# An even stream of ada rows, columns made in the middle of a block, scaled squares, and end products in two parts

## The chip, the cores and the metric

The kernel runs on one core of one Trainium2 chip. The metric is the time of one execution on the device, in microseconds. TensorE multiplies, VectorE and ScalarE work elementwise, GpSimd (POOL) does small operations and issues some DMAs, SyncE (SP) issues the others. Each engine takes its instructions in the order in which they were put into its queue and waits at an instruction until what it needs is there.

## The reference

One transformer layer on 256 tokens of width 2048, in float32. Nine vectors of 2048 (shift, scale and gate for three sublayers) come from `ada`. Each sublayer normalises its input, scales and shifts it, computes, and adds the result with a gate before a second normalisation.

```python
def _modulate(x, shift, scale):
    return _layernorm(x) * (1 + scale) + shift

def _swiglu(h, w_in, w_out):
    gate, up = jnp.split(h @ w_in, 2, axis=-1)
    return (jax.nn.silu(gate) * up) @ w_out

# in _layer
ada = (jax.nn.silu(c) @ w_ada + b_ada)[:, None, :]
sh1, sc1, g1, sh2, sc2, g2, sh3, sc3, g3 = jnp.split(ada, N_ADA, axis=-1)
h = _swiglu(_modulate(x, sh1, sc1), ffn1_w_in, ffn1_w_out)
x = _layernorm(ALPHA * x + 0.5 * (1 + g1) * h, ln1_g, ln1_b)
h = _token_mixer(_modulate(x, sh2, sc2), w_in, ...)
x = _layernorm(ALPHA * x + (1 + g2) * h, ln2_g, ln2_b)
h = _swiglu(_modulate(x, sh3, sc3), ffn2_w_in, ffn2_w_out)
x = _layernorm(ALPHA * x + 0.5 * (1 + g3) * h, ln3_g, ln3_b)
```

## The kernel before

Every matrix is split into a high part (`hi`, rounded to the fast matmul format) and the rest (`lo`). `split` makes them: ScalarE casts, VectorE subtracts (L145, L146). `mm3` then issues three products for one (L391 to L393). The 256 tokens are two row tiles of 128, a = 0 and 1. `res` holds the running x.

**The first stage** (the loop from L897) multiplies the modulated x with 24 column groups of `ffn1_w_in`, twelve of them in each of four phases j = 0 to 3. A phase uses the 512 input features 4j to 4j + 3 (in units of 128). A block n of a phase is one column group: 48 matmuls in two halves h = 0 and 1 (`first_in`, L809). Blocks other than the last add their result to `hT` on VectorE, or copy it there on ScalarE in the phase that is the first for them. The last block of a phase holds its sums in PSUM for the next phase.

The next phase needs the shift and scale of its 512 features. These are sums over 16 row blocks of `w_ada`, 512 KB each: POOL issues the load (`ar`, three buffers), VectorE multiplies by silu(c) and adds (L160; L158 for the first of them, which only multiplies). The sums lie in `acc` for j = 1 and 3 and in a part of `gate` for j = 0 and 2. `next_ada` does this in steps of two rows. At the end it transposes the sums on TensorE (L786), reduces them to columns on VectorE (L788) and adds the bias (L789). `modulate_both` (L307) normalises the 512 features on ScalarE, transposes them (L317), applies the columns on ScalarE (L322), and makes the parts `xhi` (ScalarE, L325) and `xlo` (VectorE, L327). A step of `next_ada` runs before block n for all n but 4 and 9; the one before block 11 makes the columns and finishes the modulation.

The order within an engine's queue isn't the order of the text alone. A planner issues, at each point of its own forecast, the instruction that stands first in the text among those that it takes to be ready. `tc.issue_after` puts an instruction behind a named one, and `manual_schedule` keeps VectorE in the order of the text.

**Between sublayers** (`boundary`, L572, used after the first and the second sublayer) the last output columns of both row tiles are multiplied (`last_products`), in two column halves of 256: `o` and `oh`. `add_up` adds them to x with the gate (L469 to L479, where L475 reads `oh`). Then `row_std`, `ln_affine` and `ln_stats` make the first normalisation and the mean and variance for the next one: `ln_affine` sums x in three pieces on VectorE (L541) and the squares of x minus the mean of the first piece on ScalarE (L545), with sums 7, 8 and 9. `ln_stats` puts mean and variance together on VectorE and takes the inverse root on POOL (`inv_root`, L271). POOL also multiplies it with minus the mean (L566). `modulate_tile` normalises (L339 on ScalarE; L337 on VectorE for the first tile alone), transposes (L343), applies the columns (L350, L353) and splits (L359, L360). The first products of the next sublayer (`mo` or `ge`, L664) begin with `xf` and unsplit weights.

Of the kernel before, what the change touches and what calls it, by code (L numbers as in the profile page):

```python
# [7 lines left out]
F32 = mybir.dt.float32  # L8
F32R = mybir.dt.float32r
AF = mybir.ActivationFunctionType  # L10
ALU = mybir.AluOpType
# [36 lines left out]
def layer_kernel(  # L48
# [282 lines left out]

    def modulate_tile(v, a, k0, nk, rs, xT, xs=None, on_v=False):
        ts_ = slice(a * P, (a + 1) * P)
        n = npool.tile([P, nk * P], F32, tag="n", bufs=2, name=f"n_{ntag()}")
        r = res[:, a, k0 * P:(k0 + nk) * P]
        if on_v:
            V.tensor_scalar(out=n, in0=r, scalar1=rs[:, 0:1], scalar2=rs[:, 1:2], op0=ALU.mult, op1=ALU.add)  # L337
        else:
            S.activation(n, r, AF.Identity, bias=rs[:, 1:2], scale=rs[:, 0:1])  # L339
# [82 lines left out]
    def out_proj(w, rows, nk, tag, npump, finish, before=None, turn=0, nheld=3, spare=None):  # L422
# [11 lines left out]
        for width in (1024, 512, 512):  # L434
# [16 lines left out]

            def last_products(a):
                half[a, 0] = mm_tile(f"oh_{tag}{a}")
                args = held[:-kn] + (kept if a else []) + held[-kn:]
                k0 = args[0][0] if a and kept and nu == nheld + 1 else None
                body, end = args[:-4], args[-4:]
                ends = end[0][0], end[-1][0]
                with tc.issue_after(last[0].ins) if a else nullcontext():
                    products(a, body, k0, None)
                    products(a, end, None, ends[1], w=256)  # L460
                    last.append(products(a, end, *ends, outs=half, c=256, w=256))

# [69 lines left out]
    def ln_affine(a, rs, mv, lgb, sums, sq):  # L532
# [6 lines left out]
        for i, (c0, c1) in enumerate(((0, 512), (512, 1280), (1280, 2048))):  # L539
# [3 lines left out]
            if i == 0:  # L543
                V.tensor_scalar_mul(sums[:, 4:5], sums[:, 0:1], -4.0 / D)
            S.activation(sq[:, :c1 - c0], r, AF.Square, bias=sums[:, 4:5], accum_out=sums[:, 7 + i:8 + i])  # L545
            yield


    def ln_stats(out_, sums, tag):
# [8 lines left out]
        yield  # L558
        V.tensor_scalar_add(s[2], s[2], EPS)
        yield 1  # L560
        V.tensor_scalar(out=s[6], in0=s[7], scalar1=s[8], scalar2=s[9], op0=ALU.add, op1=ALU.add)
        yield
        V.tensor_scalar(out=s[6], in0=s[6], scalar1=1.0 / D, scalar2=s[2], op0=ALU.mult, op1=ALU.add)
        yield
        inv_root(out_[:, 0:1], s[6])
# [6 lines left out]
    def boundary(products, add_up, st, lgb, v, tag, xT, entry, nk):  # L572
# [4 lines left out]
        with tc.manual_schedule(engines={mybir.EngineType.DVE}):  # L577
            products(0)
            products(1)
            for _ in add_up(0):  # L580
# [4 lines left out]
            for _ in aff[0]:  # L585
                pass
            together(lns[0])
            together(lns[0])
            m = [[modulate_tile(v, a, k, 2, mr[a], xT, xs if k < 6 else None, a + k == 0) for k in range(0, 8, 2)]
                 + [modulate_tile(v, a, k, 2, mr[a], xT) for k in range(8, nk, 2)] for a in range(2)]  # L590
            m0, m1 = m
            next(m0[0])
            next(m0[1])
            for _ in add_up(1):
# [166 lines left out]

    def next_ada(j):
        src = pair_cols(0, j)
        if j % 2:
            acc = ap.tile([P, 2, 512], F32, tag="acc", name=f"acc0_{j}")
        else:
            acc = gate[:, :1024].rearrange("p (v n) -> p v n", v=2)
        rows = []
        for k in range(0, KD + 2, 2):
            with behind(modulated[0]):  # L770
                for raw in rows:
                    ada_acc(acc, raw, k - 2 + rows.index(raw))
            rows = []
            for h in range(2 if k < KD else 0):
                raw = ap.tile([P, 2, 512], F32, tag="araw", bufs=3, name=f"ar0_{j}_{k + h}")
                G_.dma_start(raw, src[(k + h) * P:(k + h + 1) * P])
                rows.append(raw)
            if k == 10:
                mb = modulate_both(0, j, rs0, xT)
            if k in (10, 12):  # L780
                next(mb)
            yield
        js = slice(4 * j, 4 * j + 4)
        cps = aux_tile(f"cp{j}"), mm_tile(f"cq{j}")
# [4 lines left out]
        V.tensor_tensor(out=scsh[:, 0:2, js], in0=scsh[:, 0:2, js], in1=bcol[:, 0:2, js], op=ALU.add)  # L789
        for _ in mb:  # L790
            pass
        yield

# [14 lines left out]

    def first_in(j, n, i, ws):  # L809
        gu, q = i % 2, i // 2  # L810
# [5 lines left out]
        ws = list(ws)  # L816
        for h in range(2):
            for k, hi, lo in ws:
                for b, ps in enumerate(pss):
# [72 lines left out]
    with tc.manual_schedule(engines={mybir.EngineType.DVE, mybir.EngineType.Activation}):  # L892
        next(fa)
    ada["left"] = [ada_gate(2, 0, 0.5), ada_gate(2, 1, 0.5), *(ada_pair(3, j) for j in range(4)), ada_pair(6, 0),
                   ada_pair(6, 1), ada_gate(5, 0, 1.0), ada_gate(5, 1, 1.0), ada_pair(6, 2), ada_pair(6, 3),
                   ada_gate(8, 0, 0.5), ada_gate(8, 1, 0.5)]
    for j in range(4):  # L897
        fa = next_ada(j + 1) if j < 3 else load_mixer_smalls()
        for n, i in enumerate(order_of(j)):
            second = n == 1 and j == 0  # L900
            with behind(fence0[-1] if second else None), behind(high[0] if second else None):
                w = list(ws if n + j == 0 else first_w(j, i))
            for _ in range(n not in (4, 9)):
                next(fa, 0)
            with behind(fence0[-1] if second else None):
                fence0.append(first_in(j, n, i, w))
            if j == 3 and n > 2:
                pump(R_F)
# [597 lines left out]
```

## Time and profile before

| what | value |
|---|---|
| three runs | 1924.88, 1921.06, 1924.22 us; median 1924.22 |
| the profiled execution | 1923.22 us, its span 1921.5 us |
| TensorE, matmuls and weight loads | 1875.2 us and 1719.2 us busy |
| VectorE | 1463.2 us busy |
| ScalarE | 940.4 us busy |
| POOL | 56.8 us busy |
| granted TensorE clock | 0.998 |

The span runs from the first to the last instruction; the execution's own time is 1.7 us more. Matmuls overlap each other in the profile, so a wait of TensorE is best seen in the starts of the weight loads (PEld), one for each matmul. In rows of the timeline, the first column is the start, the second the duration in us, and brackets name the idle time before it and what ended it. In rows of the chain, the columns are start, duration, and what ran.

### The profile page before, as it was taken

What the parts mean: (1) busy time and instruction counts of PE and PEld (TensorE: products, weight loads), DVE (VectorE), ACT (ScalarE), POOL (GpSimd) and SP (SyncE); (2) the same over time, 40 slices, a digit from 0 to 9 for tenths busy, and PEclk for the clock granted to TensorE, in tenths of its full rate; (3) what the DMA queues carried; (4) which work ended last, traced back from release to release, by engine and by line L of the source; (5) the groups of instructions that cost most, each with busy time, mean ns of one, the idle gap of its engine ahead of it and who ended that gap; (6) DMA issues with size and microseconds to landing.
All of it is one profiled execution on the core that took longest, in us unless ns stands there. A gap on an engine that the chain in (4) does not pass through costs nothing.

```text
span 1921.5 us, 32164 instructions
## 1 busy us (share of the span) xinstructions
PE 1875.2 (98%) x13101; PEld 1719.2 (89%) x13101; DVE 1463.2 (76%) x1766; ACT 940.4 (49%) x1310; POOL 56.8 (3%) x89
## 2 busy tenths in 40 slices
PE   3999999999999999999999999999999999999997
PEld 3999999999988888698999886999999999988886
DVE  6789979777778899678787887777775654555776
ACT  5554354344354454745665544565444443544562
POOL 1211100000000000000000000000000000000000
PEclk9999999999999999999999999999999999999999
DMA  9988869999888787489878884997687656655552
GB/s 363 365 305 310 325 218 315 315 308 336 285 319 318 268 310 263 154 301 321 280 260 286 307 293 148 335 304 265 226 277 257 224 185 198 237 189 188 197 196 89
DMA packets 295867, 510.89 MB, mean 266 GB/s; under 512 B 10882, under 2 KB 159010, under 8 KB 294696
## 3 DMA queue, kind: packets, MB, share of 16 engines
q1 hardware_dynamic: 287944, 480.53, 73.4%
q0 software_dynamic: 7776, 28.32, 4.2%
q8 instruction: 102, 1.67, 0.4%
q14 instruction: 45, 0.37, 0.1%
HBM read 506.71 MB, written 2.10 MB: 265 GB/s over the span
## 4 chain that ended last, share of the span: by engine, by line
PE 89%; DVE 5%; DMA 3%; ACT 1%; issue 1%; SPq 0%; POOL 0%; DVEq 0%; ACTq 0%; POOLq 0%
PE gu_f L393 8%; PE gu_f L391 8%; PE gu_f L392 8%; PE o_f L391 8%; PE o_f L393 8%; PE o_f L392 8%; PE s L392 4%; PE s L393 4%; PE s L391 4%; DMA ar<-in_w_ada_dram 2%; PE fh L393 2%; PE fh L392 2%; PE fh L391 2%; PE fs L392 1%; PE fs L393 1%; PE fs L391 1%
## 5 line engine op out<-in xcount | busy, mean ns | idle before, releaser
L160 DVE SCALAR_TENSOR_TENSOR acc<-ar,csil,acc 128x1024 f32<-128x1024 f32 x240 | 307.5, 1281 | 33.0 <-DMA ar<-in_w_ada_dram 32.6
L392 PE MATMUL gu_f<-xlo_f,hi_f2i 128*128 128x256 f32 x768 | 212.1, 276 | 0.0
L393 PE MATMUL gu_f<-xhi_f,lo_f2i 128*128 128x256 f32 x768 | 212.1, 276 | 0.0
L391 PE MATMUL gu_f<-xhi_f,hi_f2i 128*128 128x256 f32 x768 | 212.1, 276 | 0.0
L391 PE MATMUL s<-xhi_f,hi_s 128*128 128x256 f32 x752 | 208.7, 278 | 0.7 <-ACT xhi_f L325 0.7
L392 PE MATMUL s<-xlo_f,hi_s 128*128 128x256 f32 x752 | 208.4, 277 | 0.2
L393 PE MATMUL s<-xhi_f,lo_s 128*128 128x256 f32 x752 | 207.8, 276 | 0.0
L146 DVE TENSOR_TENSOR lo_f2i<-raw_f2i,hi_f2i 128x1024 fp32r<-128x1024 f32 x96 | 117.6, 1225 | 99.8 <-ACT hi_f2i L145 99.8
L391 PE MATMUL gu_f<-xhi_f,hi_f1i 128*128 128x256 f32 x640 | 176.8, 276 | 0.0
L393 PE MATMUL gu_f<-xhi_f,lo_f1i 128*128 128x256 f32 x640 | 176.8, 276 | 0.0
L392 PE MATMUL gu_f<-xlo_f,hi_f1i 128*128 128x256 f32 x640 | 176.7, 276 | 0.0
L145 ACT CAST hi_f2i<-raw_f2i 128x1024 fp32r<-128x1024 f32 x96 | 100.8, 1050 | 137.4 <-PE gu_f L392 125.5
L145 ACT CAST hi_s<-raw_s 128x1024 fp32r<-128x1024 f32 x94 | 98.0, 1053 | 116.1 <-PE s L392 76.2
L392 PEld LDWEIGHTS gu_f<-xlo_f,hi_f2i 128*128 128x128 f32 x768 | 144.2, 188 | 0.1
L391 PEld LDWEIGHTS gu_f<-xhi_f,hi_f2i 128*128 128x128 f32 x768 | 144.2, 188 | 0.1
L393 PEld LDWEIGHTS gu_f<-xhi_f,lo_f2i 128*128 128x128 f32 x768 | 144.2, 188 | 0.0
L391 PEld LDWEIGHTS s<-xhi_f,hi_s 128*128 128x128 f32 x752 | 141.2, 188 | 1.3 <-ACT xhi_f L325 1.1
L392 PEld LDWEIGHTS s<-xlo_f,hi_s 128*128 128x128 f32 x752 | 141.3, 188 | 0.8 <-DVE xlo_f L327 0.5
L393 PEld LDWEIGHTS s<-xhi_f,lo_s 128*128 128x128 f32 x752 | 141.2, 188 | 0.0
L145 ACT CAST hi_f1i<-raw_f1i 128x1024 fp32r<-128x1024 f32 x80 | 83.4, 1050 | 116.6 <-PE gu_f L392 79.0
L145 ACT CAST hh<-hT 128x512 fp32r<-128x512 f32 x126 | 77.4, 621 | 124.6 <-PE o_f L392 124.4
L146 DVE TENSOR_TENSOR lo_f2o<-raw_f2o,hi_f2o 128x1024 fp32r<-128x1024 f32 x86 | 105.3, 1225 | 43.2 <-ACT hi_f2o L145 43.1
(503 smaller groups left out, 5433.5 us busy)
## 6 DMA issues: line engine op xcount, KB each, us to landing
ar<-in_w_ada_dram SPq DMA_DIRECT2D x240, 512.0 KB, 5.7
raw_f2i<-in_ffn_w_in_dram SPq DMA_DIRECT2D x48, 1024.0 KB, 5.1
raw_s<-in_ffn_w_in_dram SPq DMA_DIRECT2D x47, 1024.0 KB, 6.9
raw_f1o<-in_ffn_w_out_dram SPq DMA_DIRECT2D x44, 1024.0 KB, 7.5
raw_f2o<-in_ffn_w_out_dram SPq DMA_DIRECT2D x44, 1024.0 KB, 5.2
raw_f1i<-in_ffn_w_in_dram SPq DMA_DIRECT2D x40, 1024.0 KB, 7.5
ar<-in_w_ada_dram POOLq DMA_DIRECT2D x48, 512.0 KB, 6.7
raw_mxo<-in_w_out_dram SPq DMA_DIRECT2D x16, 1024.0 KB, 7.8
```

The source lines that it names most:

```text
L145: S.copy(hi, src)
L146: V.tensor_tensor(out=lo, in0=src, in1=hi.bitcast(F32), op=ALU.subtract)
L160: ins = V.scalar_tensor_tensor(out=acc, in0=raw, scalar=csil[:, k:k + 1], in1=acc, op0=ALU.mult, op1=ALU.add)
L391: PE.matmul(o, ah, bh, start=start, stop=False)
L392: PE.matmul(o, ah, bl, start=False, stop=False)
L393: return PE.matmul(o, al, bh, start=False, stop=stop)
```

## The change

Four things:

- The row loads and sums of phases 1 to 3 are one stream of 48 rows (`ada_stream`). A step issues the load of one row and the sum of the row two before it. Before a block one or two steps run: in phase 0 1, 1, 2, 2, 1, 2, 2, 1, 2, 2, 2, 1, and later two before every third block.
- The columns of the next phase are made between the two halves of block 10 (`middle`) and no longer before block 11. The normalisation and the transposes of its features stand before blocks 7 and 8 (they stood before 6 and 7), the rest of the modulation before block 11, as it did.
- The squares are scaled by 1/D within the activation. Their sums 7 and 8 are then put together with the variance's other terms on VectorE ahead of the wait, and POOL adds sum 9 just ahead of the root. The first normalised tile is (x + minus mean) times the root on VectorE, which does not use the product of L566.
- In `boundary` the end products of row tile 1 come in two parts: first all but the second column half, then, behind the normalisation and transposes of the first tile, the second half (`oh`).

```diff
-    def modulate_tile(v, a, k0, nk, rs, xT, xs=None, on_v=False):
+    def modulate_tile(v, a, k0, nk, rs, xT, xs=None, mean=None):
...
-        if on_v:
-            V.tensor_scalar(out=n, in0=r, scalar1=rs[:, 0:1], scalar2=rs[:, 1:2], op0=ALU.mult, op1=ALU.add)
+        if mean is not None:
+            V.tensor_scalar(out=n, in0=r, scalar1=mean, scalar2=rs[:, 0:1], op0=ALU.add, op1=ALU.mult)
...
-            def last_products(a):
-                half[a, 0] = mm_tile(f"oh_{tag}{a}")
+            def last_products(a, parts=(0, 1)):
+                if 0 in parts:
+                    half[a, 0] = mm_tile(f"oh_{tag}{a}")
...
-                    products(a, body, k0, None)
-                    products(a, end, None, ends[1], w=256)
-                    last.append(products(a, end, *ends, outs=half, c=256, w=256))
+                    if 0 in parts:
+                        products(a, body, k0, None)
+                        products(a, end, None, ends[1], w=256)
+                    if 1 in parts:
+                        last.append(products(a, end, *ends, outs=half, c=256, w=256))
...
-                V.tensor_scalar_mul(sums[:, 4:5], sums[:, 0:1], -4.0 / D)
-            S.activation(sq[:, :c1 - c0], r, AF.Square, bias=sums[:, 4:5], accum_out=sums[:, 7 + i:8 + i])
+                V.tensor_scalar_mul(sums[:, 4:5], sums[:, 0:1], -4.0 * D ** -1.5)
+            S.activation(sq[:, :c1 - c0], r, AF.Square, bias=sums[:, 4:5], scale=D ** -0.5, accum_out=sums[:, 7 + i:8 + i])
...
-        V.tensor_scalar_add(s[2], s[2], EPS)
+        V.tensor_scalar(out=s[6], in0=s[7], scalar1=s[2], scalar2=EPS, op0=ALU.add, op1=ALU.add)
+        yield
+        V.tensor_tensor(out=s[6], in0=s[6], in1=s[8], op=ALU.add)
         yield 1
-        V.tensor_scalar(out=s[6], in0=s[7], scalar1=s[8], scalar2=s[9], op0=ALU.add, op1=ALU.add)
-        yield
-        V.tensor_scalar(out=s[6], in0=s[6], scalar1=1.0 / D, scalar2=s[2], op0=ALU.mult, op1=ALU.add)
-        yield
+        G_.tensor_tensor(out=s[6], in0=s[6], in1=s[9], op=ALU.add)
         inv_root(out_[:, 0:1], s[6])
...
             products(0)
-            products(1)
+            products(1, (0,))
...
             next(m0[0])
+            products(1, (1,))
             next(m0[1])
...
-    def next_ada(j):
...
+    def ada_stream():
         rows = []
+        for r in range(3 * KD + 2):
+            if r >= 2:
+                with behind(modulated[0]):
+                    ada_acc(*rows.pop(0))
+            if r < 3 * KD:
+                j, k = 1 + r // KD, r % KD
+                if k == 0:
+                    sums0[j] = (ap.tile([P, 2, 512], F32, tag="acc", name=f"acc0_{j}") if j % 2 else
+                                gate[:, :1024].rearrange("p (v n) -> p v n", v=2))
+                raw = ap.tile([P, 2, 512], F32, tag="araw", bufs=3, name=f"ar0_{j}_{k}")
+                G_.dma_start(raw, pair_cols(0, j)[k * P:(k + 1) * P])
+                rows.append((sums0[j], raw, k))
             yield
...
+    def columns0(j):
+        acc, js = sums0[j], slice(4 * j, 4 * j + 4)
         cps = aux_tile(f"cp{j}"), mm_tile(f"cq{j}")
...
-    def first_in(j, n, i, ws):
+    def first_in(j, n, i, ws, middle=None):
...
         for h in range(2):
+            if h and middle:
+                middle()
...
+    rows0, smalls = ada_stream(), load_mixer_smalls()
     for j in range(4):
-        fa = next_ada(j + 1) if j < 3 else load_mixer_smalls()
...
-            for _ in range(n not in (4, 9)):
-                next(fa, 0)
+            for _ in range((1, 1, 2, 2, 1, 2, 2, 1, 2, 2, 2)[n] if j == 0 and n < 11 else 1 + ((n - 11) % 3 == 2)):
+                next(rows0, 0)
+            if j == 3:
+                next(smalls, 0)
+            elif n == 7:
+                mb = modulate_both(0, j + 1, rs0, xT)
+                next(mb)
+            elif n == 8:
+                next(mb)
+            elif n == 11:
+                for _ in mb:
+                    pass
...
-                fence0.append(first_in(j, n, i, w))
+                fence0.append(first_in(j, n, i, w, (lambda: columns0(j + 1)) if n == 10 and j < 3 else None))
```

More of the change, by code (lines that the diff above doesn't have):

```diff
@@ L588, in boundary @@
             together(lns[0])
-            m = [[modulate_tile(v, a, k, 2, mr[a], xT, xs if k < 6 else None, a + k == 0) for k in range(0, 8, 2)]
+            m = [[modulate_tile(v, a, k, 2, mr[a], xT, xs if k < 6 else None, None if a + k else sums[0][:, 5:6]) for k in range(0, 8, 2)]
                  + [modulate_tile(v, a, k, 2, mr[a], xT) for k in range(8, nk, 2)] for a in range(2)]
@@ L760, in first_ada @@
         yield
-    def next_ada(j):
[L763 to L767, printed above, removed]
-        rows = []
[L769 to L781, printed above, removed]
+    def ada_stream():
+        rows = []
+        for r in range(3 * KD + 2):
[10 more added lines that the diff above has]
+                rows.append((sums0[j], raw, k))
             yield
-        js = slice(4 * j, 4 * j + 4)
+    sums0 = {}
+    def columns0(j):
+        acc, js = sums0[j], slice(4 * j, 4 * j + 4)
         cps = aux_tile(f"cp{j}"), mm_tile(f"cq{j}")
@@ L789, in next_ada @@
         V.tensor_tensor(out=scsh[:, 0:2, js], in0=scsh[:, 0:2, js], in1=bcol[:, 0:2, js], op=ALU.add)
-        for _ in mb:
-            pass
-        yield
     NS = 12
```

## The prediction

> **What bounds the kernel now.** I read the page first (busy times, the chain that ended last), then the table of stretches, then the timeline where weight loads of TensorE (PEld rows) start late, then the chain around the ends of the first two sublayers.
>
> ```profile
> span 1921.5 us, 32164 instructions
> PE 1875.2 (98%) x13101; PEld 1719.2 (89%) x13101; DVE 1463.2 (76%) x1766; ACT 940.4 (49%) x1310; POOL 56.8 (3%) x89
> PE 89%; DVE 5%; DMA 3%; ACT 1%; issue 1%; SPq 0%; POOL 0%; DVEq 0%; ACTq 0%; POOLq 0%
> 125.00:150.00 25.00, 25.00 (x223) 25.00 (x222) 23.18 (x25) 8.94 (x9) 5.06 (x7) 1.00 0.90 316
> ```
>
> TensorE is the bound: 89% of the last chain. The matmul work is the same after the change, so only places where TensorE waits can give time back, and only new waits can cost any. The last row is a stretch of the first stage with no wait: 222 weight loads in 25 us are 0.113 us each, so a block of 48 matmuls takes 5.4 us and half of one 2.7 us. In that row VectorE is busy 23.18 of 25 us, so it has little to spare there.
>
> The first stage waits at two places, where one phase of twelve blocks passes to the next. The first:
>
> ```profile
> 89.59 1.28 DVE L160 SCALAR_TENSOR_TENSOR acc<-ar,csil,acc 128x1024 f32<-128x1024 f32 x1 [1.06 <-DMA ar<-in_w_ada_dram]
> 98.66 0.45 PEld L786 LDWEIGHTS cp<-ident,acc 128*128 128x128 f32 x4
> 100.47 1.23 DVE L146 TENSOR_TENSOR lo_s<-raw_s,hi_s 128x1024 fp32r<-128x1024 f32 x1 [1.69 <-ACT hi_s L145]
> 101.61 0.69 DVE L788 TENSOR_REDUCE scsh<-cp 128x4 f32<-128x512 f32 x1
> 102.22 0.68 DVE L788 TENSOR_REDUCE scsh<-cq 128x4 f32<-128x512 f32 x1
> 102.81 1.22 DVE L146 TENSOR_TENSOR lo_s<-raw_s,hi_s 128x1024 fp32r<-128x1024 f32 x1
> 103.94 0.17 DVE L789 TENSOR_TENSOR scsh<-scsh,bcol 128x8 f32<-128x8 f32 x1
> 104.14 1.02 ACT L322 ACTIVATE xf<-tp,scsh 128x256 f32<-128x256 f32 x2 [1.79 <-DVE scsh L789]
> 105.06 0.70 ACT L325 CAST xhi_f<-xf 128x256 fp32r<-128x256 f32 x2
> 104.89 0.19 PEld L393 LDWEIGHTS s<-xhi_f,lo_s 128*128 128x128 f32 x1
> 105.51 0.19 PEld L391 LDWEIGHTS s<-xhi_f,hi_s 128*128 128x128 f32 x1 [0.43 <-ACT xhi_f L325]
> 105.97 0.19 PEld L392 LDWEIGHTS s<-xlo_f,hi_s 128*128 128x128 f32 x1 [0.27 <-DVE xlo_f L327]
> ```
>
> The transposes of the ada columns start at 98.66, but their reductions stand behind a weight split on VectorE until 101.61, a second split follows, and ScalarE gets its columns at 104.14. TensorE needs the new input parts right after 104.89. Its steps from there are 0.62 and 0.46 where 0.11 each is normal: 0.51 + 0.35 = 0.86 us lost. The second passage is alike:
>
> ```profile
> 156.90 2.60 DVE L160 SCALAR_TENSOR_TENSOR gate<-ar,csil,gate 128x1024 f32<-128x1024 f32 x2
> 173.11 0.19 PEld L393 LDWEIGHTS s<-xhi_f,lo_s 128*128 128x128 f32 x1
> 174.01 0.19 PEld L391 LDWEIGHTS s<-xhi_f,hi_s 128*128 128x128 f32 x1 [0.71 <-ACT xhi_f L325]
> 174.47 0.19 PEld L392 LDWEIGHTS s<-xlo_f,hi_s 128*128 128x128 f32 x1 [0.27 <-DVE xlo_f L327]
> ```
>
> Steps of 0.90 and 0.46: 0.79 + 0.35 = 1.14 us. I found no such step at the third. So 0.86 + 1.14 = 2.0 us is about all that the first stage can return.
>
> The other place is the end of each of the first two sublayers. This is the chain there, in order of time, then three rows of the timeline and of one line's instructions:
>
> ```profile
> 764.56 1.25 DVE res L536 x2
> 770.75 0.20 ACT sq L545
> 770.97 0.28 DVE sums L561
> 771.27 0.22 DVE sums L563
> 771.57 0.54 POOL mr L271
> 772.20 0.20 POOL mr L566
> 772.42 0.41 DVE n L337
> 774.16 0.35 DVE oh_f L475
> 783.26 0.67 DVE xlo_mx L360 x2
> 783.93 0.20 DVE sums L561
> 784.15 0.22 DVE sums L563
> 784.45 0.54 POOL mr L271
> 785.07 0.20 POOL mr L566
> 785.29 0.61 ACT n L339
> ```
>
> ```profile
> 771.80 0.19 PEld L391 LDWEIGHTS oh_f<-hi_f1o,hh 128*128 128x128 f32 x1
> 784.39 0.19 PEld L664 LDWEIGHTS mo<-raw_mo,xf 128*128 128x128 f32 x1 [0.24 <-issue]
> 785.94 0.20 PEld L343 LDWEIGHTS tp<-ident,n 128*128 128x128 f32 x2 [1.36 <-ACT n L339]
> L271 POOL TENSOR_TENSOR rs<-mv,mhalf x4: 558/1046/1533, 764.6 to 1177.0; 128x1 f32<-128x1 f32 x4
> L271 POOL TENSOR_TENSOR mr<-sums,mhalf x4: 542/544/544, 771.6 to 1185.2; 128x1 f32<-128x1 f32 x4
> ```
>
> Row tile 0 is normalised at 772.42, row tile 1 at 785.29. TensorE has work on tile 0 until the load at 784.39 is used up, then stands 1.36 us until tile 1's transposes at 785.94. The second boundary has the same steps (the four mr roots run to 1185.2), so I price it like the first.
>
> **The change, part by part.**
>
> *Columns in the middle of block 10.* The eight transposes move from 98.66 to half a block earlier, 98.66 - 2.7 = 96.0. Their number stays, so TensorE pays nothing for them. Two reductions (0.69 and 0.68), the add (0.17) and perhaps one split (1.22) between them end 2.8 us after the transposes; these take about 0.9, so the columns stand at 96.0 + 0.9 + 2.8 = 99.7 instead of 104.1. ScalarE then needs two pairs of activations and casts, 2 x (1.02 + 0.70) = 3.4 us: 103.1, before the need at 105. Both waits go: -2.0 us. What is behind the reductions on VectorE is the split for the next blocks. VectorE now stands at them if it reaches them before 96.9, but the splits of 100.47 and 102.81 serve blocks past the passage, so they have more than a block (5.4 us) of lead. This lead is the cover; without it the wait shows on TensorE.
>
> *Even stream of rows.* The 48 loads on POOL's queue and the 48 sums on VectorE (1.28 us each) keep their number. Their program place changes from pairs in eight of twelve blocks to 19, 16 and 15 steps of one. The buffers stay three, so a load still follows the sum three rows before. In the first phase the sum of row 12 goes from block 8 to block 9, so the load of row 15 may start up to a block later. Bounds for the last sum there: its present end, 90.87, and that plus 5.4 = 96.3. The deadline is 96.0. So this costs between 0 and 0.3 us, more if rows land late; I take 0, since VectorE runs a block or two ahead of its program place. In the second phase the last two sums end at 159.5; the transposes stood one passage block (5.4) plus 0.9 before 173.2, at 166.9, and move to 164.2. That leaves 4.7 us: 0. Normalisation and the transposes of the input move one block later; they are needed only at the columns, two blocks on: 0.
>
> *Scaled squares.* Row tile 0: now 770.95 (end of the third square's sum) to 771.57 holds two VectorE operations. They become one POOL add, about 0.20 as L566, with hand-overs of 0.08 before and after (as from the end of L563, 771.49, to the root): the root starts near 771.3, so -0.3. The normalisation on VectorE no longer needs L566 (0.20 and its hand-over): another -0.26. So its result comes at 772.3 instead of 772.83. The extra VectorE operation before the wait lies beside the third square: 0. Row tile 1 still uses ScalarE and needs L566. Its two VectorE operations come behind the two xlo operations (783.26, 0.67); the POOL add need not queue there: -0.3 with no collision at all on the shared side, up to -0.65 at best.
>
> The Trainium skill, GPSIMD Engine Reference, section Specifications, says that POOL shares its SBUF interfaces with VectorE and that they collide when VectorE runs an instruction with two SBUF inputs. The trace agrees: the roots L271 take 0.54 when VectorE is idle (mr) and up to 1.53 beside the two-input L536 at 764.56 (rs). By that rule the add of tile 1 would wait for xlo.
>
> *End products in two parts.* The twelve last matmuls of tile 1 (oh, from 771.80) may stand behind the transposes of tile 0. There are two ends. If the planner puts both transposes first, TensorE stands from 771.80 to 772.3, then two transposes (0.22) and twelve matmuls at 0.12 (1.4): oh is ready about 0.2 us after the 774.1 at which L475 takes it now. The VectorE chain of tile 1 starts that much later, and of the -0.3 about -0.1 is left. If the planner keeps oh first because the transposes aren't ready, L475 comes 0.5 earlier (the VectorE chain of tile 1 starts when n is done), and with -0.3 the boundary gives -0.8. Nothing shows which; the planner issues what is ready, so a mix is nearest: -0.5 each, -1.0 for both. The later mo work shifts with tile 1, as its weights wait for buffers that tile 1's matmuls free. The third sublayer's end is not touched.
>
> Sum: -2.0 - 1.0 = -3.0 us. The profiled execution took 1923.22; 1923.22 - 3.0 = 1920.2. The median of the three runs shown is 1924.22, 1.0 above it, the mean of all four 1923.35; on that mean the sum gives 1920.3, which I take.
>
> **The rivals.**
>
> A, better: oh stays first at both boundaries and the POOL add meets no collision. Then -0.8 - 0.35 more where the add escapes xlo: about -1.1 each, -2.0 - 2.2 = -4.2, 1919.1. For it: n is ready 0.5 us after 771.80, and the planner has oh ready. Against: two-input VectorE work just there.
>
> B, last row late, a little: sum of row 15 in the first phase at 96.3 plus 1.6 for a slow landing, 1.9 us of new wait in the middle of block 10, the rest as forecast: -1.1, 1922.2. The 1.06 us that VectorE waited for a row at 89.59 speaks for it; the same late landings are in these answers on that tensor:
>
> ```profile
> DMA to landing us min/median/max: 5.9/7.0/8.6
> ```
>
> 8.6 - 7.0 is the 1.6. Against it: VectorE's lead.
>
> C, collision: both POOL steps of tile 1 take the 0.99 us more that rs shows over mr. That is +2.0 - 0.65 + 0.2 = +1.5 per boundary, so -2.0 + 3.0 = +1.0, 1924.3. Against: in the mr rows of now no root was slowed, and xlo ends after 0.67.
>
> D, slower: the deadline in the middle of a block is missed at all three passages by half a block. That is 3 x 2.7 = 8.1, with 2.0 and 1.0 gained: +5.1, 1928.4. It decides when the last sum moves from 90.87 to 98.7, 7.8 us later. The 23.18 of 25 us speak for it: VectorE recovers slowly. Against: the sums per phase are 17, 16 and 15 where they were 16 each, and 4.7 us stand free at the second passage.
>
> **How the numbers follow.** Forecast 0.48, A 0.20, B 0.14, C 0.07, D 0.11. The forecast's own range is -1.9 (boundaries at 0 but for rounding) to -4.0. About 0.2% (3.8 us, also the spread of the three runs) is what a measurement can tell from no change. Faster by more: A and a fifth of the forecast, 0.30. Slower: D, 0.11. Within: 0.59. The range reaches from A less the runs' scatter of some 1.5 us, 1917.6, to C, 1924.3; D lies outside, and a tail of A.
>
> **What would show it.** Right: no PEld step over 0.2 us at the two passages; cp transposes inside block 10 and the first L322 more than 2 us before the phase ends; the root of tile 0 within 0.4 us of the last square; tile 1's wait on ACT n under 1.36. Wrong: PEld waiting for acc or gate in the middle of block 10 (B, D); POOL mr over 0.6 or a POOL add over 0.5 (C); PEld tp waiting for n with oh behind it, and L475 late (end products at their worse end). If the time falls by much more than 4 us, I have missed a wait that my 2.0 + 2 x 1.36 doesn't hold.

## The result and the profile after

The changed kernel takes 1919.82 us (median of 19 runs, 1918.01 to 1921.79) beside 1922.61 us for the kernel before (19 runs). The ratio of the means is 0.9984 [0.9978, 0.9990], which is -3.1 us of 1922.6, with an interval of -4.2 to -1.9. A second set of runs (label again, below) gave 0.9985 [0.9976, 0.9994]. The forecast was 1920.3, a change of -3.0: the sum came out, but its terms did not.

The profiled execution took 1918.01 us, its span is 1916.3. The page's span, busy times and shares of the last chain, and the stretch of the first stage shown before:

```profile
span 1916.3 us, 32174 instructions
PE 1871.6 (98%) x13101; PEld 1717.1 (90%) x13101; DVE 1463.2 (76%) x1762; ACT 940.9 (49%) x1310; POOL 57.8 (3%) x93
PE 93%; DVE 3%; DMA 2%; ACT 1%; issue 1%; SPq 0%; POOL 0%; DVEq 0%; POOLq 0%; ACTq 0%
125.00:150.00 25.00, 25.00 (x223) 25.00 (x222) 23.71 (x26) 10.24 (x10) 4.33 (x6) 1.00 0.99 358
```

TensorE has 93% of the chain where it had 89%. A stretch without waits has the same 222 loads as before: nothing became faster, waits became fewer.

The first passage, on VectorE, and the row of the column transposes (minimum, median and maximum in ns, then first and last start):

```profile
L787 PEld LDWEIGHTS cp<-ident,acc x8: 137/138/140, 95.1 to 229.6; 128*128 128x128 f32 x8
93.54 2.35 DVE L146 TENSOR_TENSOR lo_s<-raw_s,hi_s 128x1024 fp32r<-128x1024 f32 x2
95.81 0.68 DVE L789 TENSOR_REDUCE scsh<-cp 128x4 f32<-128x512 f32 x1
96.41 0.68 DVE L789 TENSOR_REDUCE scsh<-cq 128x4 f32<-128x512 f32 x1
97.12 0.17 DVE L790 TENSOR_TENSOR scsh<-scsh,bcol 128x8 f32<-128x8 f32 x1
101.16 0.76 DVE L327 TENSOR_TENSOR xlo_f<-xf,xhi_f 128x256 fp32r<-128x256 f32 x2 [1.74 <-ACT xhi_f L325]
```

The transposes start at 95.1 instead of 98.66, the columns stand at 97.3 instead of 104.1, and the last input part is made at 101.9, some 2 us before the new phase begins. The waits of the weight loads between 36 and 246 us, first of the kernel after, then of the kernel before in the run shown, then in a further run of it (label control):

```profile
PEld s L393 <- DVE lo_first L866: 0.3, 1, 0.3
```

```profile
PEld s L391 <- ACT xhi_f L325: 1.1, 2, 0.7
PEld s L392 <- DVE xlo_f L327: 0.5, 2, 0.3
PEld s L391 <- ACT hT L829: 0.2, 1, 0.2
```

```profile
PEld s L391 <- ACT xhi_f L325: 1.1, 1, 1.1
PEld s L392 <- DVE xlo_f L327: 0.3, 1, 0.3
```

Of the kernel after only a wait at its very start is left. In the further run of the kernel before the wait at the second passage is missing, and the one at the first is longer (1.1 where the run shown has 0.43). The end of the first sublayer, in the chain in order of time, and in the weight loads and on POOL:

```profile
767.14 0.20 ACT sq L548
767.34 0.15 DVE sums L564
767.63 0.19 POOL sums L566
767.89 0.56 POOL mr L271
768.95 0.44 PE tp L343 x2
770.84 0.44 DVE oh_f L478
780.27 0.15 DVE sums L564
780.56 0.24 POOL sums L566
780.88 0.61 POOL mr L271
781.79 0.61 ACT n L339
782.45 0.45 PE tp L343 x2
```

```profile
768.09 0.19 PEld L393 LDWEIGHTS o_f<-hi_f1o,hl 128*128 128x128 f32 x1
768.95 0.20 PEld L343 LDWEIGHTS tp<-ident,n 128*128 128x128 f32 x2 [0.66 <-DVE n L337]
769.12 0.19 PEld L391 LDWEIGHTS oh_f<-hi_f1o,hh 128*128 128x128 f32 x1
770.40 0.19 PEld L393 LDWEIGHTS oh_f<-hi_f1o,hl 128*128 128x128 f32 x1
782.44 0.20 PEld L343 LDWEIGHTS tp<-ident,n 128*128 128x128 f32 x2 [1.11 <-ACT n L339]
```

TensorE now stands 0.66 us ahead of tile 0's transposes, with the twelve products of oh waiting behind them (769.12 to 770.40). L478, which was L475, comes at 770.84, that is 13.74 us after the first oh product of tile 0, where before it came 13.39 us after it: 0.35 later. In exchange tile 1's wait is 1.11 instead of 1.36.

To compare kernels I cut each span at the same instructions. All times are us. The first stage is given as the time of blocks 1 to 11 of phase 0 and the whole of phases 1, 2 and 3; a boundary runs from the first oh product of tile 0 to the last mo load (the first) or the last ge load (the second); mid is what lies between the two. The labels are those of the experiments below; control and again are the kernels before and after a second time:

```
kernel       stage 1: 0 (1-11)  1      2      3      sum   | boundary 1, 2, sum     | mid
before             62.48  68.50  67.69  66.28  264.95 | 67.44  42.54  109.98 | 333.28
control            62.95  67.70  67.50  66.32  264.47 | 67.44  42.55  109.99 | 333.12
bound_only         63.01  67.67  67.47  66.32  264.47 | 67.36  42.67  110.03 | 332.09
mid_only           63.61  67.25  68.02  65.99  264.87 | 67.40  42.55  109.95 | 331.74
mid_again          63.56  68.66  67.14  65.99  265.35 | 67.40  42.57  109.97 | 336.90
even_only          61.67  67.14  67.47  66.34  262.62 | 67.28  42.55  109.83 | 332.18
even_again         61.69  67.10  67.51  66.33  262.63 | 67.70  42.54  110.24 | 332.34
first_only         61.70  67.14  67.14  65.99  261.97 | 67.38  42.55  109.93 | 331.69
after              61.81  67.14  67.14  65.99  262.08 | 67.41  42.67  110.08 | 331.53
again              61.79  67.14  67.14  65.99  262.06 | 67.42  42.67  110.09 | 336.17
split_only         61.87  67.14  67.14  65.99  262.14 | 68.25  43.27  111.52 | 332.25
whole              61.69  67.14  67.14  65.99  261.96 | 67.00  42.21  109.21 | 332.83
improved           61.85  67.14  67.14  65.99  262.12 | 66.58  41.74  108.32 | 331.80
tile1              61.81  67.10  67.14  65.99  262.04 | 66.31  41.59  107.90 | 333.22
```

Two things are seen at once. The change has its gain in the first stage (the seven traces with the whole first-stage change have 262.0 to 262.1, the three with the first stage of before 264.5 to 265.0: -2.6 us), and the boundaries give nothing (110.0 and 110.1). And mid, which no edit touches, lies between 331.5 and 336.9 from one execution to the next, so the span of a single trace tells little: of the 5.2 us between the first two spans, 1.75 us are mid, and the two traces of the changed kernel differ by 4.6 us there.

### The profile page after: what moved, and what is told of

It is laid out like the page before. It is cut to its first block, busy times and chain, and to the rows that moved or that the text cites. A ratio compares the mean times of both kernels' runs of the same rounds, so it can differ in the third digit from the quotient of the medians.

```text
span 1916.3 us, 32174 instructions
## 1 busy us (share of the span) xinstructions
PE 1871.6 (98%) x13101; PEld 1717.1 (90%) x13101; DVE 1463.2 (76%) x1762; ACT 940.9 (49%) x1310; POOL 57.8 (3%) x93
## 4 chain that ended last, share of the span: by engine, by line
PE 93%; DVE 3%; DMA 2%; ACT 1%; issue 1%; SPq 0%; POOL 0%; DVEq 0%; POOLq 0%; ACTq 0%
PE gu_f L393 8%; PE gu_f L392 8%; PE gu_f L391 8%; PE o_f L391 8%; PE o_f L393 8%; PE o_f L392 8%; PE s L393 5%; PE s L391 5%; PE s L392 4%; PE fh L391 2%; PE fh L393 2%; PE fh L392 2%; PE fs L392 1%; PE fs L391 1%; PE fs L393 1%; PE o_mx L393 1%
```

## Experiments

**One half of the change at a time.** first_only has the first-stage change with the boundary of before, bound_only the other way round:

```diff
 first_only: after, with modulate_tile, last_products, ln_affine, ln_stats, boundary of before
 bound_only: before, with those five functions of after
```

> The kernel before with the change of the first stage alone (stream of rows and columns in the middle of block 10); boundary as before. My theory: all of the gain is here. From the first block's first matmul to the transposes of hrow (213.45 us before, 209.89 changed) it takes 209.6 to 211.0; both boundaries as before (67.4 us from the first oh to the last mo, 42.5 us from the first oh_mx to the last ge). Time against the kernel before: -2.5 to -3.5 us, ratio 0.9982 to 0.9987, the same as the whole change. Rival (each part gives its half): -2.0 or less, ratio 0.999.

> The kernel before with the squares, the first tile's normalisation and the end products in two parts alone; first stage as before. My theory: the parts cancel each other, ratio 1.000 within 0.0005; boundary 1 takes 67.3 to 67.6 us and boundary 2 42.4 to 42.8 us. Rival (the boundary pays and the trace of the changed kernel just hid it): 66.9 and 42.0, ratio 0.9995.

first_only took 1920.63 us, 0.9991 [0.9982, 0.9999], less of a gain than the 0.9982 to 0.9987 expected; bound_only 1923.18 us, 1.0010 [1.0001, 1.0019]. The table is sharper: the first stage of first_only is that of after to 0.1 us, the boundaries of bound_only are those of before to 0.1 us. The interval of bound_only begins just above no change; its trace shows no stretch that is longer, so whether the boundary change costs anything beyond these two stretches stays open.

**Which half of the first-stage change.** mid_only has the columns between the halves of block 10, the rows still in pairs; even_only has the even stream (and with it the normalisation and transposes of the input one block later, as in after), the columns before block 11 as in before:

```diff
 mid_only, against before
-    def first_in(j, n, i, ws):
+    def first_in(j, n, i, ws, middle=None):
...
         for h in range(2):
+            if h and middle:
+                middle()
...
 even_only, against first_only
             elif n == 11:
+                columns0(j + 1)
                 for _ in mb:
                     pass
...
-                fence0.append(first_in(j, n, i, w, (lambda: columns0(j + 1)) if n == 10 and j < 3 else None))
+                fence0.append(first_in(j, n, i, w))
```

> The kernel before with the columns made between the halves of block 10 alone; the rows stay in steps of two, all else as before. My theory: this is what removes the waits at the passages between phases. No weight load is late by over 0.2 us at the first and second passage; from the first matmul to the hrow transposes 210.5 to 211.5 us (213.45 before); ratio 0.9985 to 0.9992. Rival 1 (the even stream is needed, rows in pairs come late for the new deadline): TensorE waits for acc or gate in the middle of block 10, 1 us or more, and the stage takes 212.5 or more. Rival 2: the stream gives half.

> The kernel before with the even stream of rows alone; the columns stand before block 11 as before (normalisation and transposes of the input as in the changed kernel). My theory: the passages wait as before (0.86 and 1.14 us of late weight loads), the stage takes 212.5 to 213.5 us, ratio 0.9995 to 1.0003. Rival (the stream relieves the loads of the weights and VectorE, so it brings the 0.9 us by which the changed kernel was ahead before block 8): 0.7 us or more gained ahead of the first passage.

mid_only took 1923.16 us, 1.0004 [0.9995, 1.0014]; even_only 1921.28 us, 0.9993 [0.9984, 1.0002]. A second trace of each was taken:

> The columns in the middle of block 10 with rows in steps of two, profiled a second time. My theory now: the 1.69 us wait in block 5 is a late landing of weights that only sometimes happens with rows in pairs, so it comes otherwise here (0 to 2 us), while phase 2 loses again (67.7 us or more, blocks 26 and 27), since there VectorE is full and the order of its queue does it. Rival (both are set by the order): 63.6 and 68.0 us again in phases 0 and 2.

> The even stream with columns before block 11, profiled a second time. My theory now: the order of VectorE's queue takes the weights ahead of the rows, so phase 0 is 61.6 to 62.0 us again with no wait before its end, phase 1 67.14, and phases 2 and 3 keep the small steps at the passage (67.47 and 66.34). Rival (a lucky execution): phase 0 62.4 us or more.

The single executions took 1927.43 and 1920.14 us. even_only's stage 1 repeated to 0.01 us. mid_only's sum repeated within 0.5 us, but not its places: phase 2 lost nothing (67.14), against what I expected, and phase 1 lost 1.5 us instead. Against the mean of before (264.63), the even stream alone gives -2.0 and the columns alone +0.5; the columns on top of the even stream give another -0.6 (262.05 against 262.63). So the part that I had priced at nothing carries three quarters of the gain, and the part that I had priced at everything gives nothing by itself over the whole stage; mid_only's eleven timed runs show no gain either. The passages alone tell more. Blocks 10 and 11 of a phase and the first block of the next take, in us:

```
passage                     first  second  third
before                      18.32   18.59  18.33
control                     18.99   17.61  18.37
bound_only                  18.99   17.58  18.37
even_only                   17.25   17.58  18.39
even_again                  17.23   17.59  18.37
mid_only, mid_again, after  17.25   17.25  18.03
```

With the first stage of before the passages lose 2.4 to 2.7 us against after: 1.1 to 1.7 at the first, 0.3 at the third in steps too small to be listed as waits, and at the second 0.3 to 0.4 in two traces and 1.3 in one alone. So control, made to see whether the waits of 0.86 and 1.14 us repeat, shows that they do not; only their sum does, roughly. The columns in the middle of block 10 take all of this away by themselves. The stream alone takes away the loss of the first passage and leaves 0.3 at each of the others. What mid_only gains at the passages it loses again inside the phases.

Why the stream helps at the first passage is seen at its start. VectorE in a run of the kernel before (control):

```profile
41.68 2.36 DVE L146 TENSOR_TENSOR lo_s<-raw_s,hi_s 128x1024 fp32r<-128x1024 f32 x2 [2.04 <-ACT hi_s L145]
43.95 0.75 DVE L158 TENSOR_SCALAR acc<-ar,csil 128x1024 f32<-128x1024 f32 x1
44.62 1.22 DVE L146 TENSOR_TENSOR lo_s<-raw_s,hi_s 128x1024 fp32r<-128x1024 f32 x1
45.75 1.28 DVE L160 SCALAR_TENSOR_TENSOR acc<-ar,csil,acc 128x1024 f32<-128x1024 f32 x1
```

and in even_only:

```profile
41.71 2.36 DVE L146 TENSOR_TENSOR lo_s<-raw_s,hi_s 128x1024 fp32r<-128x1024 f32 x2 [1.92 <-ACT hi_s L145]
44.35 2.36 DVE L146 TENSOR_TENSOR lo_s<-raw_s,hi_s 128x1024 fp32r<-128x1024 f32 x2 [0.28 <-ACT hi_s L145]
46.63 0.75 DVE L158 TENSOR_SCALAR acc<-ar,csil 128x1024 f32<-128x1024 f32 x1
```

With rows in pairs a row sum stands between every two weight splits; with the even stream two pairs of splits go first. A split frees the buffer of the raw weights, and the next load of weights can be issued. The sixth of these loads (raw_s), in us after TensorE's first product of the stage:

```
rows in pairs:  before 19.22  control 19.39  bound_only 19.37  mid_only 19.43  mid_again 19.45
even stream:    even_only 16.34  even_again 16.50  after 16.50
```

The weights run 2.9 us further ahead of TensorE, and that lead is kept: at the passage ScalarE casts the weights at 96.97 in even_only where control waits for them until 99.51:

```profile
99.51 1.05 ACT L145 CAST hi_s<-raw_s 128x1024 fp32r<-128x1024 f32 x1 [2.45 <-DMA raw_s<-in_ffn_w_in_dram]
104.26 1.02 ACT L322 ACTIVATE xf<-tp,scsh 128x256 f32<-128x256 f32 x2 [1.78 <-DVE scsh L789]
```

```profile
96.97 1.05 ACT L145 CAST hi_s<-raw_s 128x1024 fp32r<-128x1024 f32 x1 [2.29 <-PE s L392]
101.72 1.02 ACT L322 ACTIVATE xf<-tp,scsh 128x256 f32<-128x256 f32 x2 [1.60 <-DVE scsh L787]
```

The split behind that cast stands ahead of the reductions on VectorE. With it earlier the columns, unmoved in the program, reach ScalarE 2.5 us earlier, and the list of waits of the weight loads between 36 and 246 us is empty in both traces of even_only. mid_only reaches the same by the other road: its weights are as late as those of before, but its reductions stand ahead of that split.

```profile
98.16 0.68 DVE L789 TENSOR_REDUCE scsh<-cp 128x4 f32<-128x512 f32 x1
```

So the wait at the first passage needs both, late weights and columns that stand behind their split, and either edit ends it.

mid_only keeps the short lead, and TensorE waits inside a phase, here in block 5 of phase 0:

```profile
54.45 1.28 DVE L160 SCALAR_TENSOR_TENSOR acc<-ar,csil,acc 128x1024 f32<-128x1024 f32 x1 [0.52 <-DMA ar<-in_w_ada_dram]
65.10 1.04 ACT L145 CAST hi_s<-raw_s 128x1024 fp32r<-128x1024 f32 x1 [4.27 <-DMA raw_s<-in_ffn_w_in_dram]
66.68 0.19 PEld L391 LDWEIGHTS s<-xhi_f,hi_s 128*128 128x128 f32 x1 [1.61 <-ACT hT L835]
```

VectorE waits for a row, so a split and a weight load are late; ScalarE waits for the weights, and the copy that empties PSUM stands behind that cast. The row of control at that place (53.80) came without a wait, and its copy was in time. Whether mid_only's rows land late by chance or because of the edit is not settled: in both traces that show the wait VectorE, ScalarE, POOL and SyncE run in the order of before until 30 us later, while of the three traces of before's first stage only one waits there, 0.2 us. The later waits (0.7 us in phase 2 of mid_only, 1.4 in phase 1 of mid_again) are not followed further. That the stream's longer lead is what prevents all of them is likely, since no trace with the stream has them, but not shown.

**The two boundary parts.** whole is after with the end products of tile 1 in one piece; split_only is after with the squares and the normalisation of before:

```diff
 whole, against after
-            products(1, (0,))
+            products(1)
...
-            products(1, (1,))
```

```diff
 split_only, against after (ln_stats; ln_affine and modulate_tile likewise as in before)
-        G_.tensor_tensor(out=s[6], in0=s[6], in1=s[9], op=ALU.add)
+        V.tensor_scalar(out=s[6], in0=s[7], scalar1=s[8], scalar2=s[9], op0=ALU.add, op1=ALU.add)
+        V.tensor_scalar(out=s[6], in0=s[6], scalar1=1.0 / D, scalar2=s[2], op0=ALU.mult, op1=ALU.add)
```

> The changed kernel with the end products of row tile 1 in one piece again (oh ahead of the transposes). My theory: in the changed kernel oh stands behind two transposes for which TensorE waits, L478 gets oh 0.6 us after the VectorE instruction before it has ended, and that is what takes the shorter chain's gain. With oh first, L478 follows L474 at once; each boundary is 0.5 to 0.8 us shorter than in the changed kernel (66.6 to 66.9 and 41.9 to 42.2 us). Ratio to before 0.9976 to 0.9980. Rival (the POOL add's late start is what takes the gain): boundaries within 0.2 us of the changed kernel's.

> The changed kernel with the squares, their sums and the first tile's normalisation as before; the end products in two parts stay. My theory: the transposes then wait about 0.5 us longer for the first tile, oh comes that much later, and both boundaries are longer than in either kernel: 67.9 to 68.3 and 43.1 to 43.5 us. Rival (the planner moves oh ahead of the transposes when these are late): boundaries as before.

whole took 1919.79 us, 0.9989 [0.9980, 0.9998], where 0.9976 to 0.9980 was expected; split_only, one execution, 1920.67 us. The timings can't tell whole from after; the stretches can. From the table: split products cost 0.87 us over both boundaries (110.08 against 109.21), the squares and the normalisation earn 0.78 without the split (109.99 to 109.21) and 1.44 with it (111.52 to 110.08). The two parts of the change cancel. Some times at the first boundary, in us after the first oh product of tile 0:

```
                          before  split_only  after   whole   improved  tile1
third square of tile 0 ends 10.24    10.23    10.23   10.23    10.23    10.23
root of tile 0 starts       10.88    10.87    10.79   10.79    10.67    10.67
tile 0's transposes start   12.56    12.19    11.84   12.56    12.56    12.56
L475 / L478 starts          13.39    14.08    13.74   13.04    12.92    12.92
tile 1 normalised from      24.60    25.31    24.69   23.99    23.75    23.48
tile 1's transposes start   25.25    25.96    25.34   24.64    24.40    23.95
```

In whole the oh products fill TensorE until tile 0 is normalised, and L478 comes 0.70 us earlier than in after. Everything on VectorE that leads to tile 1 moves with it. Of that the boundaries keep 0.41 and 0.46 us, a little less than the 0.5 to 0.8 expected.

**A shorter version.** In the changed kernel VectorE makes two sums while the third square runs, and the last of them ends after it. POOL's add names it as what it waited for:

```profile
767.32 0.16 DVE L564 TENSOR_TENSOR sums<-sums 128x1 f32<-128x1 f32 x1
767.14 0.19 ACT L548 ACTIVATION_READ_ACCUMULATOR sq<-res,sums 128x1 f32 x1
767.63 0.18 POOL L566 TENSOR_TENSOR sums<-sums 128x1 f32<-128x1 f32 x1 [5.05 <-DVE sums L564]
```

The square's sum ends at 767.33, L564 at 767.48, the add starts 0.15 later. improved is whole with an instruction that only the normalisation needs (minus the mean) put behind these sums; tile1 also takes the product with minus the mean out of tile 1's way:

```diff
 improved, against whole
-        V.tensor_scalar(out=s[5], in0=s[0], scalar1=s[1], scalar2=-1.0 / D, op0=ALU.add, op1=ALU.mult)
-        yield
...
         yield 1
+        V.tensor_scalar(out=s[5], in0=s[0], scalar1=s[1], scalar2=-1.0 / D, op0=ALU.add, op1=ALU.mult)
         G_.tensor_tensor(out=s[6], in0=s[6], in1=s[9], op=ALU.add)
 tile1, against improved
-  None if a + k else sums[0][:, 5:6]
+  None if k else sums[a][:, 5:6]
```

> As the run with whole end products, and the instruction that makes minus the mean (L556) moved on VectorE behind the wait, so that the sum of the first two squares is ready before the third and POOL's add starts at the third square. My theory: the POOL add starts 0.15 us earlier for each row tile; 0.1 to 0.2 us less per boundary than with whole end products alone (66.4 to 66.8 and 41.7 to 42.1 us), ratio 0.9974 to 0.9980. Rival (POOL starts late for another reason, a longer hand-over from ScalarE): the add still starts 0.3 us after the square's end, no gain over whole end products.

> As the run called improved (end products whole, minus the mean made behind the wait), and the first two columns of row tile 1 too are normalised on VectorE from the root itself, so that they don't wait for POOL's product with minus the mean. My theory: the chain of row tile 1 from the last square to its transposes sets when TensorE goes on, so it gains the product and its hand-over (0.27 us) and the shorter normalisation (0.41 us on VectorE against 0.60 on ScalarE): transposes of tile 1 0.4 us sooner after the first oh (24.0 us; 24.40 in improved, 25.25 before), boundaries 66.1 to 66.4 and 41.3 to 41.6 us; ratio to before 0.9970 to 0.9980. Rival (the transposes then wait for something else, as the end of tile 0's products): gain under 0.15 us per boundary.

improved took 1917.83 us, 0.9980 [0.9972, 0.9989]; tile1 1919.75 us, 0.9983 [0.9974, 0.9992], timed with another set of runs, beside 1924.19 us for before. The boundaries of improved are 0.89 us shorter than those of whole, more than the 0.12 us by which the root of tile 0 starts earlier: tile 1's root gains as well (its first transpose at 24.40 against 24.64, its third at 24.89 against 25.35). tile1 takes off another 0.42 over both boundaries, half of what the 0.45 by which its transposes start earlier at the first one would promise for two. The intervals of improved, tile1 and after overlap, so the timings can't tell them apart; the stretches in the traces can.

**The change again.** The changed kernel a second time, to see what repeats:

> The changed kernel a second time, as it stands, on the chip of the other runs of this call. Every reading of its first trace should come again: phases 1 and 2 of the first stage 67.14 us each, no wait over 0.2 us at a passage, boundaries 67.4 and 42.7 us; the first block (8.16 us or some 0.65 more) and the stretch between the boundaries (331.5 to 333.3) may differ. Ratio to before 0.998 to 0.999.

1921.08 us, 0.9985 [0.9976, 0.9994]. Stage 1 and the boundaries repeat to 0.02 us. Its profiled execution took 1923.26 us; 4.6 us of the difference to the first trace are in mid, which at 336.17 lies above the 331.5 to 333.3 expected. In mid VectorE meets a row that lands late; then the softmax of the second sublayer is late, and TensorE stands (waits of one stretch, the row on VectorE, TensorE's longest wait, then the granted clock in stretches, the last number but two):

```profile
PEld ptp L1128 <- ACT s L1123: 2.4, 4, 1.5
```

```profile
1092.90 1.28 DVE L160 SCALAR_TENSOR_TENSOR acc<-ar,csil,acc 128x1024 f32<-128x1024 f32 x1 [4.32 <-DMA ar<-in_w_ada_dram]
1109.44 0.14 PEld L1128 LDWEIGHTS ptp<-ident,s 128*128 128x128 f32 x1 [1.47 <-ACT s L1123]
```

```profile
1105.50:1107.00 1.50, 1.50 (x9) 1.18 (x7) 1.50 (x6) 1.01 (x5) 0.00 (x0) 1.00 0.99 363
1110.00:1111.00 1.00, 1.00 (x4) 0.86 (x4) 1.00 (x2) 0.63 (x2) 0.00 (x0) 0.51 1.02 379
1111.00:1112.00 1.00, 1.00 (x4) 0.76 (x3) 0.33 (x1) 0.00 (x0) 0.00 (x0) 0.50 1.01 360
```

## Why the prediction was right, and where it was not

**The total.** -3.0 was forecast, -3.1 [-4.2, -1.9] measured. By the stretches of the traces the changed parts give -2.6 in the first stage and +0.1 at the boundaries, -2.5 in all. The rest is within the interval. So the sum came out by luck: a term that was too small and one that was too large nearly made up for each other, 0.6 more from the stage and 1.1 less from the boundaries.

**"Columns in the middle of block 10 ... both waits go: -2.0" and "Even stream of rows ... I take 0."** At the passages the first sentence holds: both traces of mid_only lose nothing there. Its size rests on one execution: 1.14 at the second passage came in one of three traces, and the 0.3 at the third, where I had found no step, comes in all three. The step that failed is the 0 for the stream, and with it the sum of the two as separate terms. The stream alone gives -2.0 over the stage; the columns alone end with +0.5, because new waits inside the phases take back what the passages give; on top of the stream they give -0.6. I followed the chain back to the columns and stopped. The split ahead of the reductions, which stands in the rows that I quoted, waited for ScalarE's cast, and that, by name in control (2.45 us) and bound_only (2.77), for the weights' landing; in the trace that I read from, the view names the column transposes instead, which end just then. So at the first passage the term belongs as much to the order of row sums and splits as to the place of the columns. I had asked of the stream only whether its sums could come too late, not what goes ahead of them. The working of the column path was right in direction and cautious in size: columns at 99.7 forecast, at 97.3 measured, inputs at 103.1 and 101.9.

**"Scaled squares ... the root starts near 771.3, so -0.3."** It starts 0.56 us after the square's end where 0.35 was forecast (771.3 less 770.95); before it was 0.64, so the gain is 0.08. The step that failed is "the extra VectorE operation before the wait lies beside the third square: 0". It ends 0.15 after the square, and another 0.15 passes before POOL starts. improved took off another 0.12. "Another -0.26" for the normalisation was right: 11.38 against 11.72 for its start, with 0.09 of that from the root. Tile 1's -0.3 was right too: from the end of its third square to the end of its mr product 1.49 us, 1.76 before.

**"The planner issues what is ready, so a mix is nearest: -0.5 each."** There was no mix. Both boundaries have the worse end as I described it, transposes first, TensorE standing (0.66 us), then oh. For L475 I had said 0.2 later, it is 0.35, and what is left of the gain is nothing instead of -0.1. The other end, whose order whole shows, gives -0.44 and -0.33 instead of -0.8. The two ends were the right ones to name, though the better one gives half of its price; between ends that depend on an order, the middle was no choice at all.

**The rivals.** A is out: oh did not stay first, and where it does, in whole, both boundaries give -0.8, not -2.2; even tile1 stops at -2.1. B is out: no weight load waits in the middle of block 10 in seven traces with this first stage, although VectorE waits up to 2.27 us for a row some 8 us before it (2.08 in after). The last row sum of the phase begins at 89.40 in after, and at 89.59 before. C is nearly out. The POOL steps of tile 1 beside VectorE's work are 0.61 against 0.56 for tile 0's root and 0.24 against 0.19 for its add, hundredths where I had allowed 0.99 for each. The rule of the Trainium skill (GPSIMD Engine Reference, section Specifications), by which POOL collides with two-input instructions of VectorE, fits these differences in sign. As a limit it does not show here: the add runs from 780.56 while VectorE is in the two xlo operations from 780.33 to 781.08. D is out: the deadline was met at all three passages.

**The list of signs.** Right: no late step at the passages, transposes inside block 10, L322 at 97.3 long before the phase ends, tile 1's wait under 1.36. Wrong: the root within 0.4 us of the last square (0.56). The sign set for C, a POOL mr over 0.6, appears by a hundredth (0.61), without C's cost. And the sign that I had set for the worse end, PEld waiting for n with oh behind it and L475 late, is what the trace shows.

## What to carry to other kernels

A wait on the path is followed back until it ends at a transfer or at an engine that has been busy all along; the first late instruction on the way need not be the cause, and here an edit further up the same queue was worth more than the edit at the place where the wait shows. Two edits that end the same wait are not two terms of a sum. A wait read in one trace is looked for in a second one before it is priced. In a queue kept in order, try work that waits for a landing behind work that frees buffers. Where a planner decides between two orders, price both and look for what would make it choose; and leave work (here the oh products) ahead of what the engine would wait for.

## What the runs showed of the hardware that was not expected

- After four short stops within 3 us (0.26 to 1.47 us each) the granted clock of TensorE fell to 0.50 (rows above). The clock entries of that trace (again) say for how long: 3.41 us, from 1110.03 to 1113.44. Nine loads take 3.53 us there where 0.23 us each is usual, so the late softmax cost about 1.5 us on top of its wait. In the second trace of mid_only a stop of 3.1 us between two loads, up to 1083.05, did not do that.
- The Trainium skill, TensorE: Matmul & The Clock Gate, Part 1: The HAM clock gate, has the gate look at free-running windows of some 3.4 us. The traces agree with the windows: in all fourteen the clock changes between the start of the first stage and the end lie whole multiples of 3.413 us apart (in again 1071.79 us = 314 of them before the fall). So the stop up to 1083.05 lay across the edge of two windows, at 1081.85 by that trace's own entries. The same section names an idle window as the condition for the lower clock, and that does not fit: in the window before the fall TensorE was busy for 58% by the profile, and windows with 53% (first_only) and 58% (mid_again) had no such effect. What the gate counts as idle stays open.
- The first block of the first stage takes 8.1 to 8.2 or 8.7 to 8.8 us, at random over kernels. Most loads step 0.16 us or more until 3.3 to 6.5 us after the first product, then 0.11. The view of a stretch reads 1.00 in these microseconds (the kernel after, 9 loads in 2 us), but the trace's clock entries only begin where the steps change, at 38.19 in after and 40.67 in before, so this 1.00 is no measurement.

```profile
36.00:38.00 2.00, 2.00 (x11) 1.90 (x9) 1.97 (x6) 1.94 (x5) 0.00 (x0) 1.00 1.05 391
```

- Stretches without an edit differ between executions by up to 5 us, where a row load lands late and stands ahead of other work on VectorE. A difference of 3 us is seen in two dozen runs or in the same cuts of several traces, not in two spans.
